# A two-layer decoder trunk on one core: seven products for 12 instead of 8 of the 22 row tiles of the feed-forward down projection

## The chip, the core and the metric

The program runs on one core of a Trainium2 chip. The metric is the device time of one execution in microseconds (us). TensorE (PE in the profile) multiplies matrices, VectorE (DVE) and ScalarE (ACT) work on rows of numbers, GpSimd (POOL) and SyncE (SP) issue transfers (DMAs). Each engine takes the instructions of its own list in the order in which they stand there.

## What is computed

Two layers of a decoder trunk in float32, 512 tokens of 1024 features. Each layer has a feed-forward block, a mixer (a gated recurrence beside attention) and a second feed-forward block. Cut to what matters here:

```python
def swiglu(h, w_gate, w_up, w_down):
    return (jax.nn.silu(h @ w_gate) * (h @ w_up)) @ w_down      # 1024 -> 2816 -> 1024

for l in range(DEPTH):                                            # DEPTH = 2
    h = rms_norm(x, gn[0])
    x = x + 0.5 * rms_norm(swiglu(h, w_ffn1_gate[l], w_ffn1_up[l], w_ffn1_down[l]), gn[1])
    ...                                                           # the mixer
    h = rms_norm(x, gn[4])
    x = x + 0.5 * rms_norm(swiglu(h, w_ffn2_gate[l], w_ffn2_up[l], w_ffn2_down[l]), gn[5])
```

The change is in the last product, `... @ w_down`. It runs four times: two blocks in each of two layers. Its inner dimension, 2816, is 22 tiles of 128 rows.

## The kernel before

**Splitting.** A float32 operand v is held as a pair hi, lo: hi is v rounded to a shorter format (a `copy` on ScalarE, CAST in the profile), lo is the rest v - hi (a subtraction on VectorE). A product takes three matmuls: hi by hi, hi by lo, lo by hi (`mm3`, L381). In another form of the split (`split_dma`, L408) ScalarE writes hi and then -v, and a GpSimd DMA adds v to the latter as it lands; VectorE has no part in it.

**Weights.** `Stream` brings the weights through the core as a list of items. An item is 128 x 1024 numbers: it is loaded by SP into one of W32 = 4 buffers (`w32`), and split into one of WS = 6 pairs `whi`, `wlo`. `ahead` (L342) lets the split run up to `most` items ahead of the one in use; `most` is AHEAD = 3. `quarter` (L255) makes the items of the seven products; the row tiles' second column half lies beside them in tiles of the pool `big` (`b12`, `b22`).

**The down projection.** `down` (L637) multiplies the 22 activation tiles `src` (128 rows x 512 tokens) by `w_down`, into eight accumulators `y[t][h]`: t is a block of 128 tokens, h a half of the 1024 columns. A unit j is two row tiles (2j and 2j+1) of one column half; `both(j, h)` (L672) works it for the four t, 24 matmuls of 512 columns. Eight row tiles by eight accumulators can also be had by seven products of half-sized operands instead of eight (p1 to p7, sums and differences of the quarters of both operands): 8 to 15 are done so, p1 to p7 at four row tiles each.

The order of the matmuls is the program's own order:

1. the lead: units 0 to 3, h = 0, in `down`. While they run, `Late.sums` (L618) forms the activation sums of the seven products, one row pair (8 + i, 12 + i) at a time: `x1` is the split of a quarter, `quarter_sums` (L455) four VectorE instructions that give s and t, of which s is split at once and t later, in `more`. `ready` (L648) splits the row tiles of the units that follow.
2. `quarters` (L772): p1, p6, p2, p7, p5, p4, p3, 24 matmuls each.
3. units 8 to 10, h = 0; then all seven units with h = 1, of which the last four (TAIL) go token block by token block, so that the norm of block t can start while t + 1 is multiplied.
4. while the last block is multiplied, `pre.turn` (L572) transposes the first two normed blocks for the stage that follows.

What sets the order elsewhere: TensorE's list is as written. The other engines' lists are ordered when the program is built, by a scheduler with priorities and a timing model of its own; instructions given to `pin` keep the order in which they are written among each other. Tiles are slots of pools (`big`: 61 slots; accumulators: `acc` 5, `aux` 3), and an instruction that takes a slot waits for the slot's last user.

Of the kernel before, what the change touches and what calls it, by code (L numbers as in the profile page):

```python
# [15 lines left out]
P = 128  # L16
# [22 lines left out]
LEAD = 8  # L39
ORDER = ("p1", "p6", "p2", "p7", "p5", "p4", "p3")  # L40
DMAS = ()
# [4 lines left out]
def trunk(ctx: ExitStack, tc: tile.TileContext, xin, wall, gains, lbT, hgain, sinks, c_dist, c_mask, c_ident, out):  # L46
# [109 lines left out]
    class Stream:  # L156
# [36 lines left out]
        def rows(self, kt, fast):  # L193

            u0 = self.wall

            def pieces(j, h):
                b = [(4 * h + i) * kt + 2 * j for i in range(4)]  # L200
                return [(slice(i * 2 * P, (i + 1) * 2 * P), wall[u0 + n // 8][:, n % 8 * P : (n % 8 + 2) * P]) for i, n in enumerate(b)]

            def unit(j, h):
                c = 2 * j * P
                self.src[self.n] = [(None, wall[u0 + 4 * h : u0 + 4 * h + 4, :, c : c + 2 * P].rearrange("u p c -> p u c"))] if kt == 8 else pieces(j, h)
                self.plain(1)

            j0, later = LEAD // 2 if fast else 0, []
            if fast:
                for j in range(j0):  # L210
                    unit(j, 0)

                u = self.n
                for q in range(2):
                    self.src[u + q] = pieces(j0 + q, 0)
                    self.src[u + 2 + q] = pieces(j0 + 2 + q, 0)
                self.side[u + 1] = [pieces(j0 + q, 1) for q in range(4)]
                for k in ORDER:
                    for q in range(2):
                        it = Item(k, u + q + (2 if k in ("p2", "p4") else 0), 4)  # L220
                        it.base, it.q = u, q
                        self.items.append(it)
                self.t2 = [None, None]
                self.n += 4
                for j in range(j0):
                    later.append(j)
                j0 += 4
            for j in range(j0, kt // 2):
                unit(j, 0)
                later.append(j)  # L230
            for j in later:
                unit(j, 1)
            self.wall = u0 + kt

        def load(self, upto):
            while self.dma < min(upto, self.n):
                w = sb.tile([P, D], F32, tag="w32", name=nm("w32"), bufs=W32)
                u = self.dma
                if isinstance(self.src[u], list):
                    for c, a in self.src[u]:  # L240
                        nc.sync.dma_start(w.rearrange("p (m c) -> p m c", m=4) if c is None else w[:, c], a)  # L241
                else:
                    for c in (slice(0, D // 2), slice(D // 2, D)) if u == 0 else (slice(0, D),):
                        nc.sync.dma_start(w[:, c], wall[self.src[u]][:, c])
                self.raw[u] = w
                self.dma += 1
                if u in self.side:
                    self.b12, self.b22 = [], []
                    for i, ps in enumerate(self.side[u]):
                        v = [big(), big()]  # L250
                        for c, a in ps:
                            nc.sync.dma_start(v[c.start // S][:, c.start % S : c.start % S + 2 * P], a)
                        (self.b22 if i > 1 else self.b12).append(v)

        def quarter(self, it):  # L255

            self.load(it.base + 4)
            q, h = it.q, (slice(0, S), slice(S, D))
            if it.kind in ("p1", "p2", "p5", "p4"):
                w = [self.raw[it.u][:, c] for c in h]  # L260
                if it.kind == "p4":
                    for c in range(2):
                        pin(nc.vector.tensor_tensor(w[c], w[c], self.t2[q][c], op=ALU.add))
            elif it.kind == "p6":

                t = sb.tile([P, D], F32, tag="tt", name=nm("tt"), bufs=2)
                self.t2[q] = w = [t[:, c] for c in h]
                for c in range(2):
                    t1 = self.raw[it.u][:, h[c]]
                    pin(nc.vector.tensor_tensor(t1, t1, self.b12[q][c], op=ALU.subtract))  # L270
                    pin(nc.vector.tensor_tensor(w[c], t1, self.b22[q][c], op=ALU.subtract))
            elif it.kind == "p3":
                w = self.b22[q]
            elif it.kind == "p7":

                w = self.b12[q]
                for c in range(2):
                    pin(nc.vector.tensor_tensor(w[c], w[c], self.b22[q][c], op=ALU.add))
            it.hi = sb.tile([P, D], F32R, tag="whi", name=nm("whi"), bufs=WS)
            it.lo = sb.tile([P, D], F32R, tag="wlo", name=nm("wlo"), bufs=WS)  # L280
            for c in range(2):
                nc.scalar.copy(it.hi[:, h[c]], w[c])  # L282
                if it.kind in DMAS:
                    nc.scalar.mul(it.lo[:, h[c]], w[c], -1.0)
                    nc.gpsimd.dma_start(it.lo[:, h[c]].bitcast(F32), w[c], accum_op=ALU.add)
                else:
                    nc.vector.tensor_tensor(it.lo[:, h[c]], w[c], it.hi[:, h[c]].bitcast(F32), op=ALU.subtract)  # L287
            self.done += 1
            self.flight += 1
            if it.kind in ("p5", "p4"):  # L290
# [106 lines left out]
    def split(src, scale=None, to=None):  # L397

        hi, lo = to or (big(F32R), big(F32R))
        if scale is None:  # L400
            nc.scalar.copy(hi, src)  # L401
# [70 lines left out]
    class Quarters:  # L472
# [4 lines left out]
        def operand(self, n):  # L477
# [4 lines left out]
            return [[v[:, i, :] for v in x[k]] for k in range(4)]  # L482
# [127 lines left out]
    class Late(Quarters):  # L610


        def __init__(self, src, k0):
            self.src, self.k0 = src, k0
            self.x1, self.x56, self.x37, self.t = [], [], [], []
# [12 lines left out]
        def more(self, n):  # L628

            for i in range(len(self.x37), n):  # L630
                self.src[self.k0 + 4 + i] = split(self.src[self.k0 + 4 + i])
                self.x37.append(pair_split(self.t[i], split_dma))

        def raw(self, half, i):
            return [cut(self.src[self.k0 + 4 + k], HALF[half]) for k in range(4)] if i else self.x1

    def down(src, kt, l, n, nxt, fast):  # L637
# [8 lines left out]
        pre = Pre(*nxt) if nxt else None  # L646

        def ready(n):  # L648

            for i in range(min(n, kt)):  # L650
# [6 lines left out]
        def piece(b, t, h, j, i):  # L657
            st = cut(src[2 * j + i], slice(t * P, (t + 1) * P))
            mm3(y[t][h], st, [halves(w, i) for w in b[2:]], 2 * j + i == 0 and not (fast and h and t < 2), 2 * j + i == kt - 1)
# [20 lines left out]
        js = list(range(kt // 2))  # L680
        if fast:
            late = Late(src, LEAD)
            for j in range(LEAD // 2):
                ready(2 * j + EARLY)
                while len(late.x56) < min(4, 8 * (j + 1) / LEAD):
                    late.sums()
                both(j, 0)
            more = quarters(late, y)
            del js[LEAD // 2 : LEAD // 2 + 4]
        for j in js[LEAD // 2 if fast else 0 :]:  # L690
            ready(2 * j + 2 + EARLY)
            both(j, 0)
        if not fast:
            for t in range(TT):
                y[t][1] = aux() if t > 1 else acc()
        fetch()
        last = js[-TAIL:]
        for j in js[:-TAIL]:
            both(j, 1)

        warm = small([P, 1], "warm", 2)
        pin(nc.scalar.activation(out=warm, in_=src[last[0]][0][:, :1].bitcast(F32), func=AF.Sqrt, bias=eps_t, scale=0.0))
# [69 lines left out]
    def quarters(late, y):  # L772
# [3 lines left out]
        def product(n, o, start, stop=True):  # L776
            its = [ws.whole(), ws.whole()]
            for k in range(4):
                for t in range(2):
                    st = cut(late.operand(n)[k], slice(t * P, (t + 1) * P))  # L780
                    it = its[k // 2]
                    mv = [w.rearrange("p (m two c) -> p m two c", two=2, c=P)[:, :, k % 2, :] for w in (it.hi, it.lo)]
                    mm3(o[t], st, mv, start and k == 0, stop and k == 3)
# [12 lines left out]
        late.more(2)  # L796
        p = product(1, two(acc), True)
        p1, u2, u3, c12, c22 = (two(big) for _ in range(5))
        for t in range(2):
            nc.scalar.copy(p1[t], p[t])  # L800
        late.more(4)
# [8 lines left out]
        product(4, [y[t][0] for t in (2, 3)], False, False)  # L810
        for t in range(TT):
            y[t][1] = aux() if t > 1 else acc()
        product(3, [y[t][1] for t in (0, 1)], True, False)
# [72 lines left out]
    def fast(pre, a, start):  # L886
        def early():
            if j == FT - 1:
                for i in range(EARLY):
# [562 lines left out]
```

## Time and profile before

| what | value |
| --- | --- |
| time, median of 3 runs (lowest, highest) | 2100.54 us (2100.14, 2103.34) |
| the profiled execution's own time | 2100.66 us |
| its span, first to last instruction | 2098.9 us |
| PE busy, instructions | 2090.3 us, 13549 |
| DVE busy, instructions | 1550.5 us, 2705 |
| ACT busy, instructions | 1122.4 us, 1899 |
| POOL busy, instructions | 154.2 us, 188 |
| mean granted TensorE clock | 0.999 |

How to read it: a row of the timeline gives start and duration in us, engine, line, operation, what is written and read, the shape, how many were merged, and in brackets the engine's idle time before it and what ended that. A duration is from start to end, and instructions of an engine overlap a little: the distance between two starts is what one costs in a queue. Matmuls overlap most: their ends are modelled, so a busy share near 100% does not mean that every matmul starts as early as it can.

### The profile page before, as it was taken

What the parts mean: (1) busy time and instruction counts of PE and PEld (TensorE: products, weight loads), DVE (VectorE), ACT (ScalarE), POOL (GpSimd) and SP (SyncE); (2) the same over time, 40 slices, a digit from 0 to 9 for tenths busy, and PEclk for the clock granted to TensorE, in tenths of its full rate; (3) what the DMA queues carried; (4) which work ended last, traced back from release to release, by engine and by line L of the source; (5) the groups of instructions that cost most, each with busy time, mean ns of one, the idle gap of its engine ahead of it and who ended that gap; (6) DMA issues with size and microseconds to landing.
All of it is one profiled execution on the core that took longest, in us unless ns stands there. A gap on an engine that the chain in (4) does not pass through costs nothing.

```text
span 2098.9 us, 35207 instructions
## 1 busy us (share of the span) xinstructions
PE 2090.3 (100%) x13549; PEld 1875.3 (89%) x13549; DVE 1550.5 (74%) x2705; ACT 1122.4 (53%) x1899; POOL 154.2 (7%) x188
## 2 busy tenths in 40 slices
PE   9999999999999999999999999999999999999998
PEld 8899988887888999998899998898778989999987
DVE  5877886766776777789587778767687758777884
ACT  6555564456454555556455556554653545555562
POOL 0011000000000011110001110000000000111000
PEclk9999999999999999999999999999999999999999
DMA  8577653312236357774447775632122563677651
GB/s 246 152 181 184 178 157 135 111 61 71 71 101 203 127 122 182 181 198 122 154 114 176 183 181 150 191 120 92 51 81 61 136 193 103 159 182 181 184 160 51
DMA packets 148071, 298.35 MB, mean 142 GB/s; under 512 B 16992, under 2 KB 74816, under 8 KB 147904
## 3 DMA queue, kind: packets, MB, share of 16 engines
q1 hardware_dynamic: 122416, 228.16, 33.2%
q0 software_dynamic: 25344, 67.91, 18.7%
q8 instruction: 106, 1.74, 0.3%
q14 instruction: 61, 0.50, 0.1%
q10 hardware_dynamic: 144, 0.05, 0.0%
HBM read 213.43 MB, written 14.73 MB: 109 GB/s over the span
## 4 chain that ended last, share of the span: by engine, by line
PE 88%; DMA 0%; DVE 0%; ACT 0%; SPq 0%; issue 0%; ACTq 0%
PE acc L115 64%; PE aux L115 22%; PE aux L125 1%; PE acc L125 1%; DMA wlo<-w 0%; DMA w<-wall 0%; SPq L241 0%; DVE s L402 0%; ACT whi L282 0%; DVE s L731 0%; ACT s L600 0%; DVE s L712 0%; DVE s L896 0%; DVE wlo L287 0%; ACT m L895 0%
## 5 line engine op out<-in xcount | busy, mean ns | idle before, releaser
L115 PE MATMUL acc<-s,whi 128*128 128x256 f32 (+1 forms) x4952 | 1059.3, 311 | 0.4 <-ACT whi L325 0.3
L115 PEld LDWEIGHTS acc<-s,whi 128*128 128x128 f32 x4952 | 808.0, 191 | 51.3 <-issue 3.2
L115 PE MATMUL acc<-s,wlo 128*128 128x256 f32 (+1 forms) x2476 | 766.6, 310 | 0.1
L115 PEld LDWEIGHTS acc<-s,wlo 128*128 128x128 f32 x2476 | 472.6, 191 | 25.0 <-DVE wlo L332 0.4
L325 ACT CAST whi<-w 128x1024 fp32r<-128x1024 f32 (+1 forms) x341 | 316.6, 948 | 237.6 <-PE acc L115 95.5
L115 PE MATMUL acc<-whi,s 128*128 128x512 f32 x1264 | 413.6, 393 | 0.1
L325 ACT CAST whi<-tt 128x1024 fp32r<-128x1024 f32 x154 | 161.4, 1048 | 326.5 <-DVE tt L319 184.2
L332 DVE TENSOR_TENSOR wlo<-w,whi 128x1024 fp32r<-128x1024 f32 (+1 forms) x181 | 218.3, 1215 | 151.4 <-ACT whi L325 149.6
L115 PEld LDWEIGHTS acc<-whi,s 128*128 128x128 f32 x1264 | 237.1, 188 | 54.7 <-ACT whi L325 1.6
L332 DVE TENSOR_TENSOR wlo<-tt,whi 128x1024 fp32r<-128x1024 f32 x154 | 188.1, 1221 | 98.8 <-ACT whi L325 98.7
L115 PE MATMUL acc<-wlo,s 128*128 128x512 f32 x632 | 246.4, 390 | 0.0
L115 PE MATMUL aux<-s,whi 128*128 128x256 f32 (+1 forms) x1248 | 230.4, 285 | 0.0
L330 POOL DMA_DIRECT2D wlo<-w x160 | 137.8, 863 | 1258.6 <-ACT wlo L329 704.9
L115 PE MATMUL aux<-whi,s 128*128 128x512 f32 x592 | 196.7, 390 | 0.0
L115 PEld LDWEIGHTS aux<-s,whi 128*128 128x128 f32 x1248 | 195.2, 192 | 1.1 <-issue 0.5
L115 PE MATMUL aux<-s,wlo 128*128 128x256 f32 (+1 forms) x624 | 177.5, 284 | 0.0
L115 PEld LDWEIGHTS acc<-wlo,s 128*128 128x128 f32 x632 | 118.7, 188 | 23.4
L115 PEld LDWEIGHTS aux<-whi,s 128*128 128x128 f32 x592 | 111.1, 188 | 22.8
L329 ACT ACTIVATE wlo<-w 128x1024 fp32r<-128x1024 f32 (+1 forms) x160 | 129.8, 844 | 0.0
L401 ACT CAST s<-s 128x512 fp32r<-128x512 f32 (+1 forms) x164 | 88.4, 580 | 71.5 <-DVE s L460 67.9
L115 PEld LDWEIGHTS aux<-s,wlo 128*128 128x128 f32 x624 | 119.8, 192 | 0.3
L115 PE MATMUL aux<-wlo,s 128*128 128x512 f32 x296 | 115.2, 389 | 0.0
(186 smaller groups left out, 2128.6 us busy)
## 6 DMA issues: line engine op xcount, KB each, us to landing
w<-wall SPq DMA_DIRECT2D x267, 512.0 KB, 3.7
wlo<-w POOLq DMA_DIRECT2D x83, 512.0 KB, 5.5
w<-wall SPq DMA_DIRECT2D x288, 128.0 KB, 3.3
wlo<-w POOLq DMA_DIRECT2D x77, 256.0 KB, 3.3
x_d<-s SPq DMA_DIRECT2D x48, 256.0 KB, 2.1
s<-x_d SPq DMA_DIRECT2D x48, 256.0 KB, 5.5
w<-wall SPq DMA_DIRECT2D x34, 256.0 KB, 3.0
s<-wall SPq DMA_DIRECT2D x64, 128.0 KB, 3.6
```

The source lines that it names most:

```text
L115: nc.tensor.matmul(o, lhsT, rhs, start=start, stop=stop)
L125: nc.tensor.transpose(o, src, ident)
L325: i = nc.scalar.copy(it.hi[:, c], w[:, c])
L329: nc.scalar.mul(it.lo[:, c], w[:, c], -1.0)
L330: nc.gpsimd.dma_start(it.lo[:, c].bitcast(F32), w[:, c], accum_op=ALU.add)
L332: nc.vector.tensor_tensor(it.lo[:, c], w[:, c], it.hi[:, c].bitcast(F32), op=ALU.subtract)
L401: nc.scalar.copy(hi, src)
```

## The change

- The seven products take row tiles 0 to 11 (SEVEN = 12, six row tiles to a product) instead of 8 to 15. The lead is now units 6 to 10 (five, row tiles 12 to 21) with h = 0; no unit with h = 0 comes after the products. With h = 1 the same five units follow, the last four again block by block.
- The products come as p1, p3, p7, p2, p6, p4, p5, with other sums: p1 is added to p6 and p7 at the end, and p3, p2, p4 go straight to accumulators, with three items (36 matmuls) each.
- In the lead `most` is 1 (the item in use and one more), except at its last unit. ScalarE's roundings are pinned there: weights, `x1` and the row tiles of the lead stand on ScalarE in the order in which they are written. The row tiles that the lead splits (`part`) are given up after their unit and split again for h = 1.
- Of the sums, t is split in the lead by `split_dma`; s and the raw row tiles 6 to 11 after p7, also by `split_dma`. Before, s was split in the lead with VectorE.
- y[2][1] and y[3][1] are now `acc`, y[0][1] and y[1][1] `aux`.
- The first four row tiles of the lead are split ahead of it, as before (now tiles 12 to 15).

```diff
-LEAD = 8
-ORDER = ("p1", "p6", "p2", "p7", "p5", "p4", "p3")
+SEVEN = 12
+ORDER = ("p1", "p3", "p7", "p2", "p6", "p4", "p5")
...
         def quarter(self, it):
-            self.load(it.base + 4)
...
+            n, q, h = SEVEN // 4, it.q, (slice(0, S), slice(S, D))
+            self.load(it.base + n if it.kind == "p3" else it.u + 1)
...
             for c in range(2):
-                nc.scalar.copy(it.hi[:, h[c]], w[c])
...
+                i = nc.scalar.copy(it.hi[:, h[c]], w[c])
+                if self.pinned:
+                    pin(i)
+                pin(nc.vector.tensor_tensor(it.lo[:, h[c]], w[c], it.hi[:, h[c]].bitcast(F32), op=ALU.subtract))
...
     class Late(Quarters):
         def sums(self):
-            k = self.k0 + len(self.x56)
-            a = [self.src[i][:, c] for i in (k, k + 4) for c in HALF]
+            k = len(self.x1)
+            a = [self.src[i][:, c] for i in (k, k + self.n) for c in HALF]
             x = big(F32R, [P, 2, S // 2])
-            self.x1.append(split(a[0], to=(x[:, 0, :], x[:, 1, :])))
+            self.x1.append(split(a[0], to=(x[:, 0, :], x[:, 1, :]), hold=pin))
             s, t = quarter_sums(a[0], a[2], a[1], a[3], True)
-            self.x56.append(pair_split(s))
-            self.t.append(t)
+            self.s.append(s)
+            self.x37.append(pair_split(t, split_dma))
             self.src[k] = ()
...
         if fast:
-            late = Late(src, LEAD)
-            for j in range(LEAD // 2):
-                ready(2 * j + EARLY)
-                while len(late.x56) < min(4, 8 * (j + 1) / LEAD):
+            late = Late(src)
+            ws.pinned = True
+            for i, j in enumerate(js):
+                ws.most = 1 if j != js[-1] else AHEAD
+                for k in range(2 * j, min(2 * j + EARLY, kt)):
+                    if k not in part and not isinstance(src[k], tuple):
+                        part[k] = split(src[k], hold=pin)
+                while len(late.x1) < min(late.n, (late.n * (i + 1) + 3) // 4):
                     late.sums()
                 both(j, 0)
-            more = quarters(late, y)
+                for k in (2 * j, 2 * j + 1):
+                    part.pop(k, None)
+            ws.pinned = False
+            more = quarters(late, y, fetch)
...
     def quarters(late, y, fetch):
-        add(u2, product(6, two(aux), True), p1)
-        product(2, [y[t][0] for t in (0, 1)], False, False)
-        add(u3, product(7, two(acc), True), u2)
-        p = product(5, two(aux), True)
-        add(c12, p, u2)
+        product(3, [y[t][1] for t in (0, 1)], True, False)
+        p = product(7, two(acc), True)
+        late.rest()
+        late.more()
+        add(u3, p, p1)
+        product(2, [y[t][0] for t in (0, 1)], False)
+        p = product(6, two(acc), True)
+        add(c12, p, p1)
+        add(u3, p, u3)
+        product(4, [y[t][0] for t in (2, 3)], False)
+        fetch()
+        p = product(5, two(acc), True)
         add(c22, p, u3)
+        add(c12, p, c12)
```

Three places show how the lists move. First ScalarE in the lead, where the weights of a unit are rounded. Before, from the weights of the lead's fourth and last unit (`whi_490`) on; the `L282` rows are the first items of p1, `m_464` is the SiLU of the last gate tile, which ends the stage before, and the rest are activations:

```order
L325 CAST whi_490_2836<-w32_456_2665 128x1024
L401 CAST s_474_2749<-s_108_578 128x512
L282 CAST whi_503_2894<-w32_467_2710 128x512 x2
L282 CAST whi_514_2945<-w32_478_2760 128x512 x2
L895 ACTIVATE m_464_2702<-m_464_2702 128x512
L401 CAST s_498_2875<-s_217_1157 128x256
L401 CAST s_501_2884<-s_499_2878 128x512
L401 CAST s_505_2918<-s_139_711 128x512
L401 CAST s_507_2922<-s_157_804 128x512
```

Now, the same list at the end of the lead's roundings; `whi_535` is the fifth unit's weights, `s_538` and `s_540` its two row tiles (20 and 21), the `L408`/`L409` pairs the split of t (`s_527` and `s_532` for sums 4 and 5 of the six), 256-wide casts the `x1`:

```order
L398 CAST s_521_2985<-s_417_2427 128x512
L398 CAST s_523_2989<-s_437_2560 128x512
L398 CAST s_525_2993<-s_108_578 128x256
L408 CAST s_528_3002<-s_527_2997 128x512
L409 ACTIVATE s_529_3003<-s_527_2997 128x512
L398 CAST s_530_3007<-s_139_711 128x256
L408 CAST s_533_3016<-s_532_3011 128x512
L409 ACTIVATE s_534_3017<-s_532_3011 128x512
L322 CAST whi_535_3027<-w32_467_2710 128x1024
L398 CAST s_538_3054<-s_457_2693 128x512
L398 CAST s_540_3058<-s_497_2880 128x512
```

The weights of the fifth unit stand behind the roundings of five of the six sums; before, the weights of all the lead's units and of p1's two items stood ahead of the sums.

Second, VectorE where the stage before ends (`m_464` again). Before:

```order
L875 TENSOR_TENSOR m_464_2702<-acc_459_2697,s_462_2700 128x2x256
L287 TENSOR_TENSOR wlo_504_2895<-w32_467_2710,whi_503_2894 128x512 x2
L287 TENSOR_TENSOR wlo_515_2946<-w32_478_2760,whi_514_2945 128x512 x2
L877 TENSOR_TENSOR s_463_2701<-acc_460_2698,m_464_2702 128x512
L882 TENSOR_TENSOR m_464_2702<-acc_460_2698,s_463_2701 128x256
L883 TENSOR_TENSOR m_464_2702<-aux_461_2699,s_463_2701 128x512
L896 SCALAR_TENSOR_TENSOR s_493_2868<-m_464_2702 128x512
```

and now:

```order
L891 TENSOR_TENSOR m_464_2702<-acc_459_2697,s_462_2700 128x2x256
L893 TENSOR_TENSOR s_463_2701<-acc_460_2698,m_464_2702 128x512
L898 TENSOR_TENSOR m_464_2702<-acc_460_2698,s_463_2701 128x256
L899 TENSOR_TENSOR m_464_2702<-aux_461_2699,s_463_2701 128x512
L912 SCALAR_TENSOR_TENSOR s_497_2880<-m_464_2702 128x512
L399 TENSOR_TENSOR s_502_2887<-s_80_440,s_502_2887 128x256
L456 TENSOR_TENSOR s_503_2890<-s_177_901,s_80_440 128x256
```

The four subtractions for p1's items have left this place; the sums follow at once.

Third, TensorE where the down projection ends and the next stage starts with four accumulators. Before, from the last matmul of y[3][1] (`aux_603`) on:

```order
L115 MATMUL aux_603_3390<-whi_646_3637,s_621_3454 128x512
L115 MATMUL acc_730_3963<-s_694_3854,whi_666_3691 128x256
L115 MATMUL acc_730_3963<-s_695_3855,whi_666_3691 128x256
L115 MATMUL acc_730_3963<-s_694_3854,wlo_667_3692 128x256
L115 MATMUL acc_731_3964<-s_694_3854,whi_666_3691 128x256
```

and now:

```order
L114 MATMUL acc_662_3695<-whi_667_3710,s_690_3761 128x512
L114 MATMUL acc_759_4052<-s_723_3943,whi_695_3780 128x256
L114 MATMUL acc_759_4052<-s_724_3944,whi_695_3780 128x256
L114 MATMUL acc_759_4052<-s_723_3943,wlo_696_3781 128x256
L114 MATMUL acc_760_4053<-s_723_3943,whi_695_3780 128x256
```

y[3][1] now sits in one of the five `acc`, and the next stage's fourth accumulator, `acc_762`, takes its slot.

More of the change, by code (lines that the diff above doesn't have):

```diff
@@ L276, in quarter @@
                 w = self.b12[q]
-                for c in range(2):
-                    pin(nc.vector.tensor_tensor(w[c], w[c], self.b22[q][c], op=ALU.add))
+                sums(w, w, self.b22[q], ALU.add)
+            elif it.kind == "p6":
+                w = self.t2[q]
+            else:
+                w = raw
+                sums(w, w, self.t2[q], ALU.add)
             it.hi = sb.tile([P, D], F32R, tag="whi", name=nm("whi"), bufs=WS)
@@ L395, in cut, with split @@
         return pair[0][:, c], pair[1][:, c]
-    def split(src, scale=None, to=None):
+    def split(src, scale=None, to=None, hold=lambda i: i):
         hi, lo = to or (big(F32R), big(F32R))
         if scale is None:
-            nc.scalar.copy(hi, src)
+            hold(nc.scalar.copy(hi, src))
             nc.vector.tensor_tensor(lo, src, hi.bitcast(F32), op=ALU.subtract)
@@ L481, in operand @@
             x, i = (self.x56, n - 5) if n in (5, 6) else (self.x37, (n - 3) // 4)
-            return [[v[:, i, :] for v in x[k]] for k in range(4)]
+            return [[v[:, i, :] for v in p] for p in x]
     class First(Quarters):
@@ L646, in down @@
         pre = Pre(*nxt) if nxt else None
+        js = list(range(SEVEN // 2 if fast else 0, kt // 2))
+        part = {}
         def ready(n):
-            for i in range(min(n, kt)):
+            for i in range(2 * js[0], min(n, kt)):
                 if not isinstance(src[i], tuple):
@@ L657, in piece @@
         def piece(b, t, h, j, i):
-            st = cut(src[2 * j + i], slice(t * P, (t + 1) * P))
-            mm3(y[t][h], st, [halves(w, i) for w in b[2:]], 2 * j + i == 0 and not (fast and h and t < 2), 2 * j + i == kt - 1)
+            k = 2 * j + i
+            st = cut(part.get(k) or src[k], slice(t * P, (t + 1) * P))
+            start, stop = k == 2 * js[0], k == kt - 1
+            if fast:
+                start, stop = start and (h == 0 or t > 1), stop and h == 1
+            mm3(y[t][h], st, [halves(w, i) for w in b[2:]], start, stop)
         xt = [[None] * 2 for _ in range(TT)]
@@ L678, in both @@
                 order.poll()
-        js = list(range(kt // 2))
         if fast:
-            late = Late(src, LEAD)
-            for j in range(LEAD // 2):
-                ready(2 * j + EARLY)
-                while len(late.x56) < min(4, 8 * (j + 1) / LEAD):
+            late = Late(src)
[6 more added lines that the diff above has]
+                while len(late.x1) < min(late.n, (late.n * (i + 1) + 3) // 4):
                     late.sums()
                 both(j, 0)
-            more = quarters(late, y)
[L689 to L696, printed above, removed]
+                for k in (2 * j, 2 * j + 1):
+                    part.pop(k, None)
+            ws.pinned = False
+            more = quarters(late, y, fetch)
+        else:
+            for j in js:
+                ready(2 * j + 2 + EARLY)
+                both(j, 0)
+            fetch()
+        for t in range(TT):
+            if not y[t][1]:
+                y[t][1] = (acc if (t > 1) == fast else aux)()
         last = js[-TAIL:]
         for j in js[:-TAIL]:
+            ready(2 * j + 2 + EARLY)
             both(j, 1)
         warm = small([P, 1], "warm", 2)
-        pin(nc.scalar.activation(out=warm, in_=src[last[0]][0][:, :1].bitcast(F32), func=AF.Sqrt, bias=eps_t, scale=0.0))
+        pin(nc.scalar.activation(out=warm, in_=src[2 * last[0]][0][:, :1].bitcast(F32), func=AF.Sqrt, bias=eps_t, scale=0.0))
         left = [TT]
@@ L770, in down, with quarters @@
         return pre
-    def quarters(late, y):
+    def quarters(late, y, fetch):
         def product(n, o, start, stop=True):
-            its = [ws.whole(), ws.whole()]
-            for k in range(4):
+            x = late.operand(n)
+            for k in range(late.n):
+                if k % 2 == 0:
+                    it = ws.whole()
+                mv = [w.rearrange("p (m two c) -> p m two c", two=2, c=P)[:, :, k % 2, :] for w in (it.hi, it.lo)]
                 for t in range(2):
[L780 to L783, printed above, removed]
+                    mm3(o[t], cut(x[k], slice(t * P, (t + 1) * P)), mv, start and k == 0, stop and k == late.n - 1)
                     ws.used((it, 1))
@@ L794, in two @@
             return [f(), f()]
-        late.more(2)
         p = product(1, two(acc), True)
-        p1, u2, u3, c12, c22 = (two(big) for _ in range(5))
+        late.x1 = None
+        p1, u3, c12, c22 = (two(big) for _ in range(4))
         for t in range(2):
             nc.scalar.copy(p1[t], p[t])
-        late.more(4)
-        add(u2, product(6, two(aux), True), p1)
-        product(2, [y[t][0] for t in (0, 1)], False, False)
-        add(u3, product(7, two(acc), True), u2)
-        p = product(5, two(aux), True)
-        add(c12, p, u2)
+        for t in range(2):
+            y[t][1] = aux()
+        product(3, [y[t][1] for t in (0, 1)], True, False)
[8 more added lines that the diff above has]
+        product(4, [y[t][0] for t in (2, 3)], False)
+        fetch()
+        p = product(5, two(acc), True)
         add(c22, p, u3)
[L810 to L813, printed above, removed]
+        add(c12, p, c12)
         return [[(p1, u3)[t // 2][t % 2], (c12, c22)[t // 2][t % 2]] for t in range(TT)]
@@ L888, in early @@
             if j == FT - 1:
-                for i in range(EARLY):
+                for i in range(SEVEN, SEVEN + EARLY):
                     a[i] = split(a[i])
```

96 lines of the change are left out of this document (43 added, 53 removed).

## The prediction

> **What bounds the kernel now.** I read the page first: the share of each engine, then the chain that ended last, then TensorE's waits.
>
> ```profile
> PE 2090.3 (100%) x13549; PEld 1875.3 (89%) x13549; DVE 1550.5 (74%) x2705; ACT 1122.4 (53%) x1899; POOL 154.2 (7%) x188
> PE 88%; DMA 0%; DVE 0%; ACT 0%; SPq 0%; issue 0%; ACTq 0%
> PE acc L125 <- DVE s L731: 2.9, 1, 2.9
> PE aux L115 <- DVE eps_t L138: 1.1, 1, 1.1
> PE acc L115 <- ACT whi L325: 0.3, 1, 0.3
> ```
>
> TensorE is the bound: it waits three times in the whole program, 4.3 us together, at the start and the end. So a matmul taken away is worth its full time, and a wait put anywhere into TensorE's list costs its full length. The question is whether VectorE and ScalarE still deliver in time. That is read in the timeline around one down projection; I use the first, whose lead starts at 240.94. Call that time T.
>
> ```profile
> 240.94 0.40 PE L115 MATMUL acc<-whi,s 128*128 128x512 f32 x1
> 251.85 0.44 PE L115 MATMUL acc<-whi,s 128*128 128x512 f32 x1
> 252.60 0.74 PE L115 MATMUL acc<-whi,s 128*128 128x512 f32 x2
> 263.16 0.39 PE L115 MATMUL acc<-whi,s 128*128 128x512 f32 x1
> 274.04 0.39 PE L115 MATMUL acc<-whi,s 128*128 128x512 f32 x1
> 284.92 0.39 PE L115 MATMUL aux<-whi,s 128*128 128x512 f32 x1
> ```
>
> From 263.16 (start of p1) to 274.04 and 284.92 there are 48 matmuls of 512 columns each: 10.88 us, so **0.2267 us a matmul**. The lead's 96 would end at T + 21.76 = 262.70; p1 starts at 263.16, so the lead loses 0.46 us already, at its third unit (251.85 to 252.60), where the rows' splits are just late. There is no slack in the lead before, and that is where the change adds work.
>
> **What is removed.** A down before has 16 row tiles at 24 matmuls, halves of both columns counted (14 units at 24 = 336), and 7 x 24 = 168 for the products: 504. Now 10 units (240) and 7 x 36 = 252: 492. Twelve fewer in each of four downs, 48 in all: 4 x 12 x 0.2267 = **-10.88 us**. "TensorE: Matmul & The Clock Gate" of the Trainium skill, section "Wait — 56ns, not 53.3ns?", gives 215.7 ns from start to start for 512 columns on a warm array; by it the 48 would be worth 10.35 us, and the rows here are 5% above it.
>
> **The lead, step by step.** Two engines hand the sums back and forth. VectorE, around the end of the stage before and the first sum:
>
> ```profile
> 242.52 0.69 DVE L875 TENSOR_TENSOR m<-acc,s 128x512 f32<-128x512 f32 x1
> 243.12 1.28 DVE L287 TENSOR_TENSOR wlo<-w,whi 128x512 fp32r<-128x512 f32 x2
> 244.67 1.39 DVE L287 TENSOR_TENSOR wlo<-w,whi 128x512 fp32r<-128x512 f32 x2 [0.27 <-ACT whi L282]
> 245.98 0.68 DVE L877 TENSOR_TENSOR s<-acc,m 128x512 f32<-128x512 f32 x1
> 246.70 0.42 DVE L882 TENSOR_TENSOR m<-acc,s 128x256 f32<-128x256 f32 x1
> 247.04 0.68 DVE L883 TENSOR_TENSOR m<-aux,s 128x512 f32<-128x512 f32 x1
> 248.47 0.69 DVE L896 SCALAR_TENSOR_TENSOR s<-m 128x512 f32<-128x512 f32 x1 [0.76 <-ACT m L895]
> 249.08 0.42 DVE L402 TENSOR_TENSOR s<-s,s 128x256 fp32r<-128x256 f32 x1
> 249.42 0.42 DVE L459 TENSOR_TENSOR s<-s,s 128x256 f32<-128x256 f32 x1
> 250.09 0.42 DVE L460 SCALAR_TENSOR_TENSOR s<-s,s 128x256 f32<-128x256 f32 x1
> 250.54 0.42 DVE L462 TENSOR_TENSOR s<-s,s 128x256 f32<-128x256 f32 x1
> 240.78 1.23 DVE L332 TENSOR_TENSOR wlo<-w,whi 128x1024 fp32r<-128x1024 f32 x1 [1.24 <-ACT whi L325]
> 241.92 0.69 DVE L402 TENSOR_TENSOR s<-s,s 128x512 fp32r<-128x512 f32 x1
> ```
>
> By the distances of starts VectorE takes 0.60 for 512 numbers (248.47 to 249.08), 0.34 for 256 (249.08 to 249.42), 0.45 where the next one reads its result (250.09 to 250.54), 0.71 so for 512 (L877 to L882), and 1.14 for 1024. ScalarE:
>
> ```profile
> 239.70 1.05 ACT L325 CAST whi<-w 128x1024 fp32r<-128x1024 f32 x1 [2.19 <-PE aux L115]
> 240.65 0.61 ACT L401 CAST s<-s 128x512 fp32r<-128x512 f32 x1
> 247.81 0.63 ACT L895 ACTIVATE m<-m 128x512 f32<-128x512 f32 x1 [2.47 <-DVE m L883]
> 248.35 0.39 ACT L401 CAST s<-s 128x256 fp32r<-128x256 f32 x1
> 250.60 1.97 ACT L401 CAST s<-s 128x512 fp32r<-128x512 f32 x4 [1.86 <-DVE s L460]
> 258.45 0.93 ACT L401 CAST s<-s 128x512 fp32r<-128x512 f32 x2 [1.96 <-DVE s L460]
> 264.89 0.62 ACT L411 CAST s<-s 128x512 fp32r<-128x512 f32 x1
> 265.41 0.63 ACT L412 ACTIVATE s<-s 128x512 fp32r<-128x512 f32 x1
> ```
>
> ScalarE takes 0.95 for 1024, 0.52 for 512, 0.31 for 256 (0.93 for one of each, the last at its full 0.39). It starts 0.09 after VectorE's result (250.09 + 0.42 to 250.60), VectorE 0.03 after ScalarE's (247.81 + 0.63 to 248.47).
>
> With these I play the new lists through:
>
> 1. The four L287 are gone from VectorE's place between L875 and L877. L877 can start 0.71 after L875, at 243.23 instead of 245.98: **2.75 us earlier**. L883 ends at 244.97, the SiLU runs from 245.06, and sum 0 is done at 248.21 (249.08 to 250.96 takes 1.88, from 246.33).
> 2. Then each sum is a loop: t's two roundings on ScalarE (0.09 + 0.52 + 0.52), x1 of the next sum, which stands behind them (0.39 + 0.03), and on VectorE x1's rest, L457 and L459 (0.34 + 0.45 + 0.42). 2.76 us. Sum 1 is done at 250.97.
> 3. Row tiles 16 and 17 stand between t and the next x1: two roundings more (1.04) and two subtractions. ScalarE rounds t from 251.06, the tiles at 252.10 and 252.62, and VectorE subtracts until 253.44 and 254.04. TensorE wants them for its third unit at T + 10.88 = 251.82. Its first matmul needs the rounding that ends at 252.72, the third the first rest, and this unit starts **1.23 late**.
> 4. Sum 2 is done at 255.85 (4.88 with two tiles between). Tiles 18 and 19 follow, rounded by 258.1; the fourth unit starts at 251.82 + 1.23 + 5.44 = 258.49, with its first tile rounded at 257.6: in time, by some 0.6 with the rests.
> 5. Sum 3 is done at 260.71, sum 4 at 263.47. Only then come t's two roundings, and behind them the **weights of the fifth unit**, pinned there because `most` is 1: 264.60 to 265.65. Tile 20 is rounded by 266.17; VectorE's rest of the weights ends at 266.92, those of tiles 20 and 21 at 267.52 and 268.12.
> 6. TensorE wants the fifth unit at 262.70 + 1.23 = 263.93. The six matmuls of its first token block follow these results one by one, the last after 268.12, so the block ends at 268.49; without any wait in the lead it would end at 262.70 + 6 x 0.2267 = 264.07. **The lead loses 4.42 us** and had lost 0.46: +3.96 a down. The bounds: if sums 2 to 4 each ran 0.3 shorter, 3.5; each 0.3 longer, 5.3.
> 7. The sixth sum (VectorE done 269.9) and t's roundings stand ahead of p1's weights. ScalarE rounds them from 271.02, VectorE's second half of the rest ends at 272.97, and TensorE asks for it at 268.49 + 18 x 0.2267 + 0.23 = 272.80: **+0.27** with the 0.09 for the handover. Bounds 0 and 0.6, since a few tenths of lateness in 6 shift the asking too.
>
> After p1 each product has 36 x 0.2267 = 8.16 us of TensorE's time for three items (6 casts, 3.1 us, and 6 to 18 subtractions, 3.6 to 10.8 us), and the heavier ones, p7 and p6, are followed by p2 and p5 or p4, that need less. Played through, operands of p3 to p5 stand ready 3 us and more ahead, so I cost the products' additions, the six raw tiles and six s by GpSimd (12 transfers off VectorE's list) and the loads on SP at nothing. If that cover were gone by 1 us in one product it would cost 4 us in all. The row tiles that are split twice (six, 6 x 0.60 on VectorE) fall between h = 1 units of 5.44 us: nothing, too.
>
> **The turn.** Three downs are followed by a stage with four `acc` at once.
>
> ```profile
> 357.42 0.40 PE L115 MATMUL acc<-s,whi 128*128 128x256 f32 x2
> 357.77 0.40 PE L115 MATMUL acc<-s,whi 128*128 128x256 f32 x2
> 358.23 0.68 DVE L712 TENSOR_TENSOR s<-aux,s 128x512 f32<-128x512 f32 x1
> ```
>
> Before, y[3][1] is in `aux`, and VectorE's read of it, ending at 358.91, holds nobody up. Now it is in `acc`, and the next stage's fourth accumulator takes its slot. TensorE asks after nine matmuls, at 357.42 + 9 x 0.12 = 358.50 (three take 0.35). The read ends 0.41 after that at the least, and 1.4 after if VectorE, with the re-splits in its tail, is 1 us later. I take **+0.65**, nearer the first, since the old row is the only one shown; three times, +1.95. After the last down no stage follows.
>
> **The sum.** Per down -2.72 + 3.96 + 0.27 = +1.51, four times +6.04; the turn +1.95; together +8.0. The profiled execution took 2100.66, 0.12 from the median of 2100.54, so 2108.7 by the one and 2108.5 by the other: **2108.6 us**.
>
> **Rivals.**
>
> *Faster: the lead keeps up.* The removed 10.88 and the old loss of 4 x 0.46 = 1.84 come back, and p1 is on time: about 2088. For it speaks that VectorE starts the sums 2.75 us earlier. It decides at the fifth unit's weights: they would have to be rounded some 3 us earlier, before sum 3's roundings. The list has them behind sum 4's, and 2.76 a sum follows from rows alone. Chance 0.08.
>
> *No change.* If half of the lead's wait is hidden (x1 and t taking less of the loop than the rows say) and the turn costs 0.4: 4 x (-2.72 + 1.98 + 0.1) + 1.2 = -1.4, so 2099; up to 2104 with the turn at its upper end. Chance 0.12.
>
> *Slower still: the clock.* TensorE waits over 2 us before the fifth unit and has only six matmuls in the next 2 us. The end of the program shows what a pause does:
>
> ```profile
> 2093.23 1.63 PE L125 MATMUL acc<-ident,s 128*128 128x128 f32 x8 [2.85 <-DVE s L731]
> 2094.00:2095.00 1.00, 0.86 (x4) 0.45 (x4) 0.62 (x1) 0.10 (x1) 0.00 (x0) 0.61 0.00 0
> 2095.00:2096.00 1.00, 0.00 (x0) 0.00 (x0) 0.00 (x0) 0.48 (x1) 0.00 (x0) 0.50 0.38 121
> ```
>
> After a wait of 2.85 us the granted clock falls to 0.61 and 0.50, some 3.8 us after the last dense matmul. If it did so in the lead and stayed at half for as long, 1.9 us of work would be lost each time: four times 7.6, about 2116. Against it: the pause is shorter, and the old profile has no other such slice. Chance 0.12. "TensorE: Matmul & The Clock Gate" of the Trainium skill, section "What's actually happening", says that the clock drops to half after an idle window of about 3.4 us and comes back after a busy one as long; by that rule the drop needs a longer pause than the one I work out, and one trip would cost about 1.7 us. The trace's end agrees with the drop to half.
>
> That the change does not do what it says can be left out: twelve matmuls a down are gone from TensorE's list.
>
> **Chances and range.** The main case has 0.68, its own range 2105 to 2113 from the bounds of 6, 7 and the turn. The range 2101 to 2116 adds the upper half of "no change" and the clock; outside lie the faster rival and the tails. No change means within 0.2%, 4.2 us, about what a measurement of this kernel tells apart: 0.12. Faster 0.08, slower 0.80.
>
> **What would show it.** In the new profile, TensorE's waits should name row splits (ACT L398, DVE L399) and the fifth unit's weights (DVE L329) in four places, 4 us and more together at each; the weights' cast L322 should start some 23.7 us after the lead's start; p1 should start near T + 31.6, where five units without a loss (120 matmuls) would make T + 27.2; a small wait on DVE L725 should stand at the next stage's start, three times; matmuls should number 13501. The prediction is wrong if p1 starts before T + 29, or if waits show in the products, or if slices of the granted clock go below 9.

## The result, and the profile after

| | before | after |
| --- | --- | --- |
| time, median | 2100.91 us (4 runs, 2100.14 to 2103.34) | 2125.53 us (4 runs, 2124.27 to 2127.51) |
| ratio, 95% interval | | 1.0116, 1.0099 to 1.0134 |
| profiled execution: span | 2098.9 us | 2123.5 us |
| matmuls | 13549 | 13501 |

The change makes the kernel 24.6 us slower; 8.0 were forecast. The page of the changed kernel, with the chain, and its TensorE waits (line: us in total, times, longest):

```profile
PE 2095.3 (99%) x13501; PEld 1869.7 (88%) x13501; DVE 1589.3 (75%) x2801; ACT 1181.4 (56%) x2035; POOL 202.6 (10%) x244
PE 68%; DVE 7%; ACT 5%; DMA 3%; issue 2%; SPq 1%; ACTq 0%; DVEq 0%; POOL 0%; POOLq 0%
PE acc L114 <- ACT s L398: 12.9, 8, 2.7
PE aux L114 <- DVE s L399: 4.1, 7, 0.8
PE acc L114 <- DVE s L588: 1.1, 3, 0.4
PE acc L114 <- DVE wlo L329: 0.9, 4, 0.2
```

PE's busy time rises by 5.0 us with 48 matmuls fewer: the busy share does not show the slow clock (6.3 us, below), nor all of a stop, since a matmul alone counts as 0.39 us and one in a dense row costs 0.2267. The chain leaves TensorE for VectorE, ScalarE and loads, which it hardly did before.

**The lead** (first down, T = 241.16; PE, then ScalarE around the fifth unit):

```profile
253.11 0.50 PE L114 MATMUL acc<-whi,s 128*128 128x512 f32 x1 [0.88 <-ACT s L398]
266.83 0.51 PE L114 MATMUL acc<-whi,s 128*128 128x512 f32 x1 [2.23 <-ACT s L398]
267.57 0.50 PE L114 MATMUL acc<-wlo,s 128*128 128x512 f32 x1 [0.23 <-DVE wlo L329]
264.18 0.62 ACT L408 CAST s<-s 128x512 fp32r<-128x512 f32 x1 [1.59 <-DVE s L459]
265.23 1.03 ACT L322 CAST whi<-w 128x1024 fp32r<-128x1024 f32 x1
266.17 1.44 ACT L398 CAST s<-s 128x512 fp32r<-128x512 f32 x3
```

The third unit waits for row splits, the fifth for its weights and rows, which ScalarE rounds at T + 24.07 and T + 25.01, behind t of the fifth sum. This is the forecast place (T + 23.7 for the weights).

**The clock.** One-microsecond windows of the second down, busy us (count) of PE, PEld, DVE, ACT, POOL, then the granted clock:

```profile
968.00:969.00 1.00, 0.41 (x1) 0.19 (x1) 0.95 (x1) 1.00 (x4) 0.24 (x1) 1.00 0.24 43
969.00:970.00 1.00, 0.76 (x3) 0.25 (x2) 1.00 (x3) 0.37 (x2) 0.00 (x0) 0.79 1.08 186
970.00:971.00 1.00, 1.00 (x3) 0.81 (x4) 1.00 (x3) 0.00 (x0) 0.00 (x0) 0.50 0.68 170
972.00:973.00 1.00, 1.00 (x4) 0.80 (x3) 0.28 (x1) 0.64 (x2) 0.00 (x0) 0.50 0.59 166
973.00:974.00 1.00, 1.00 (x6) 0.77 (x5) 0.00 (x0) 1.00 (x3) 0.20 (x1) 1.00 0.00 0
```

After the fifth unit's wait the clock is at half from 969.58 (0.79 is 0.42 us at half) to 973.0, although TensorE works again: these windows touch three or four matmuls each, 973:974 at full clock six.

**The units with h = 1** (first down; PE, then ScalarE; last the fourth down's ScalarE):

```profile
342.46 0.73 PE L114 MATMUL aux<-whi,s 128*128 128x512 f32 x2 [0.78 <-DVE s L399]
344.20 0.73 PE L114 MATMUL aux<-whi,s 128*128 128x512 f32 x2 [0.78 <-DVE s L399]
331.70 1.05 ACT L322 CAST whi<-w 128x1024 fp32r<-128x1024 f32 x1 [5.12 <-DMA w<-wall]
335.98 1.05 ACT L322 CAST whi<-w 128x1024 fp32r<-128x1024 f32 x1 [1.62 <-DMA w<-wall]
336.94 2.18 ACT L398 CAST s<-s 128x512 fp32r<-128x512 f32 x4
339.02 1.04 ACT L322 CAST whi<-w 128x1024 fp32r<-128x1024 f32 x1
339.96 1.13 ACT L398 CAST s<-s 128x512 fp32r<-128x512 f32 x2
2086.76 3.21 ACT L398 CAST s<-s 128x512 fp32r<-128x512 f32 x6
```

The six row tiles that are split a second time are rounded from 336.94 on, behind weights whose loads are late. TensorE goes block by block there and asks for all six within one block of 5.4 us, from 336.2. In the fourth down they are rounded in one go, and nothing waits.

**The turn:**

```profile
366.17 0.47 PE L114 MATMUL acc<-s,whi 128*128 128x256 f32 x2 [0.35 <-DVE s L588]
366.67 0.50 PE L114 MATMUL acc<-s,whi 128*128 128x256 f32 x2
365.94 0.68 DVE L725 TENSOR_TENSOR s<-acc,s 128x512 f32<-128x512 f32 x1
```

The next stage starts at 364.95 with three matmuls to an accumulator. The third accumulator (366.17) waits for L588, which writes the rest half of a normed block from an accumulator. The fourth starts at 366.67, as soon as L725 has read its slot (365.94 + 0.68 = 366.62). That is 0.64 after 364.95 + 9 x 0.12, and 0.66 in the other two turns. The list of waits names L588 alone, because before the fourth accumulator hardly any idle time is left; but L725 comes last, and by itself it would hold TensorE to the same point.

**Where 24.6 us come from.** I list each matmul's start against the one before, less 0.2267 us (0.12 for 256 columns), and add what is over 0.1:

| down | lead | slow clock | h = 1 | turn | down, start to end, after less before |
| --- | --- | --- | --- | --- | --- |
| 1 | 4.8 | 1.55 | 3.5 | 0.6 | 123.79 - 116.48 = +7.3 |
| 2 | 4.2 | 1.54 | 1.9 | 0.6 | 121.47 - 116.06 = +5.4 |
| 3 | 4.7 | 1.59 | 1.05 | 0.6 | 121.09 - 116.16 = +4.9 |
| 4 | 5.7 | 1.59 | 0 | none | +4.7 |
| sum | 19.4 | 6.3 | 6.4 | 1.8 | 22.3 |

19.4 + 6.3 + 6.4 less the 10.9 of the removed matmuls and 0.5 that the old leads lost is 20.7 of the 22.3; most of the rest is slips under 0.1 us. With the turns' 1.8 it is 24.1 of 24.6.

### The profile page after: what moved, and what is told of

Its sections match the earlier page's. It is cut to its first block, busy times and chain, and to the rows that moved or that the text cites. A ratio compares the mean times of both kernels' runs of the same rounds, so it can differ in the third digit from the quotient of the medians.

```text
span 2123.5 us, 35581 instructions
## 1 busy us (share of the span) xinstructions
PE 2095.3 (99%) x13501; PEld 1869.7 (88%) x13501; DVE 1589.3 (75%) x2801; ACT 1181.4 (56%) x2035; POOL 202.6 (10%) x244
## 4 chain that ended last, share of the span: by engine, by line
PE 68%; DVE 7%; ACT 5%; DMA 3%; issue 2%; SPq 1%; ACTq 0%; DVEq 0%; POOL 0%; POOLq 0%
PE acc L114 52%; PE aux L114 14%; DMA w<-wall 3%; DVE wlo L329 1%; PE aux L124 1%; DVE wlo L277 1%; ACT whi L322 1%; ACT s L409 1%; ACT s L408 1%; DVE s L399 1%; ACT whi L274 1%; SPq L233 1%; DMA s<-s 1%; DVE s L255 0%; PE acc L124 0%
## 5 line engine op out<-in xcount | busy, mean ns | idle before, releaser
L114 PE MATMUL acc<-whi,s 128*128 128x512 f32 x1344 | 443.1, 397 | 13.2 <-ACT s L398 12.9
L322 ACT CAST whi<-w 128x512 fp32r<-128x512 f32 (+1 forms) x325 | 299.6, 942 | 175.5 <-PE acc L114 107.9
L114 PEld LDWEIGHTS acc<-whi,s 128*128 128x128 f32 x1344 | 253.9, 189 | 76.7 <-ACT s L398 16.3
L329 DVE TENSOR_TENSOR wlo<-w,whi 128x1024 fp32r<-128x1024 f32 (+1 forms) x165 | 199.0, 1214 | 103.0 <-ACT whi L322 102.2
L114 PE MATMUL acc<-wlo,s 128*128 128x512 f32 x672 | 264.3, 393 | 0.9 <-DVE wlo L329 0.9
L114 PE MATMUL aux<-whi,s 128*128 128x512 f32 x480 | 161.6, 395 | 4.1 <-DVE s L399 4.1
L114 PEld LDWEIGHTS acc<-wlo,s 128*128 128x128 f32 x672 | 127.3, 189 | 27.7 <-DVE wlo L329 2.2
L114 PEld LDWEIGHTS aux<-whi,s 128*128 128x128 f32 x480 | 90.1, 189 | 26.4 <-DVE s L399 7.8
L399 DVE TENSOR_TENSOR s<-s,s 128x512 fp32r<-128x512 f32 (+1 forms) x148 | 86.8, 620 | 27.2 <-ACT s L398 27.1
L912 DVE SCALAR_TENSOR_TENSOR s<-m 128x512 f32<-128x512 f32 x69 | 47.8, 692 | 76.1 <-ACT m L911 75.7
```

What stands on the lines that cost most here:

```text
L114: nc.tensor.matmul(o, lhsT, rhs, start=start, stop=stop)
L322: i = nc.scalar.copy(it.hi[:, c], w[:, c])
L329: nc.vector.tensor_tensor(it.lo[:, c], w[:, c], it.hi[:, c].bitcast(F32), op=ALU.subtract)
L399: nc.vector.tensor_tensor(lo, src, hi.bitcast(F32), op=ALU.subtract)
L912: nc.vector.scalar_tensor_tensor(z, m[:, 0:2, :], -1.0, m[:, 2:4, :], op0=ALU.mult, op1=ALU.mult)
```

## Experiments

Theory 2 is the prediction's: the sums fill ScalarE and VectorE, and what stands behind five of them is late. Theory 1 blames only the weights' place. The re-splits and the clock are asked after separately.

**Weights three items ahead**

```diff
-                ws.most = 1 if j != js[-1] else AHEAD
+                ws.most = AHEAD
```

> The changed kernel, with the weights of the lead rounded three items ahead instead of one (`most` = AHEAD in the whole lead); the sums stay where they are. Theory 1 (the fifth unit waits because its weights stand behind five sums): its weights come early, the wait of 3.3 us there and the drop of the clock behind it go, four downs gain 4 x (3 to 5), about 2107. Theory 2 (it waits because the sums, 2.76 us each and 4.9 with two row tiles, fill ScalarE and VectorE; whatever stands behind five of them is late, and row tiles 20 and 21 stand there too): the weights' roundings go in ahead of the early sums and push everything behind them, so the third unit loses some 2.5 instead of 1.3, the fifth still 3.3; 2125 to 2132.

Measured 2127.52 us (2 runs), as theory 2 has it. From start to start the four leads lose 24.5 us instead of 19.4. TensorE's wait for row splits grows, and ScalarE in the first lead shows why:

```profile
PE acc L114 <- ACT s L398: 16.2, 8, 2.7
251.56 1.03 ACT L322 CAST whi<-w 128x1024 fp32r<-128x1024 f32 x1
252.50 1.44 ACT L398 CAST s<-s 128x512 fp32r<-128x512 f32 x3
```

The fifth unit's weights are in time at 251.56, but go ahead of the third unit's rows, and the fifth unit still waits for its own. The weights' place by itself is not the cause; theory 1 falls.

**Sums late**

```diff
-                ws.most = 1 if j != js[-1] else AHEAD
+                ws.most = AHEAD
...
-                while len(late.x1) < min(late.n, (late.n * (i + 1) + 3) // 4):
+                while len(late.x1) < (1, 1, 2, 4, 6)[i]:
```

> The changed kernel with `most` = AHEAD and the six sums put off: 1, 1, 2, 4, 6 of them formed by the lead's units 1 to 5 instead of 2, 3, 5, 6, 6. Theory 2 (too many sums ahead of the fifth unit's operands): no wait in the lead, so the drop of the clock behind it does not come either; each down gains 4.0 to 4.5 and 1.6: 2101 to 2104, with the waits for the split-again row tiles at h = 1 still there. Theory 3 (the lead's roundings are late because ScalarE's fixed order waits for something else, a load or the accumulator): the waits stay, within 3 us of the changed kernel's 2125.5.

Measured 2109.95 us (4 runs; ratio to before 1.0043, 1.0026 to 1.0059), 15.6 less than the changed kernel, but 6 us above the 2101 to 2104 expected. The wait for row splits in the lead is gone from the list; what stands there:

```profile
PE aux L114 <- DVE s L399: 5.6, 10, 0.8
PE acc L114 <- DVE wlo L277: 1.8, 6, 0.3
```

The four leads lose 0.7 us together, and the granted clock drops once, after the h = 1 waits of the third down, instead of four times. But of 24.1 us (lead 19.4, three slow clocks 4.7) 8.5 are given back. TensorE comes some 5 us earlier now; from start to start it loses 9.5 instead of 6.4 us at h = 1 and, new, 4.8 in the products. (The rows above, 5.6 and 1.8, count only what shows as idle.) With the 0.7 left in the leads that is about the 8.5. Since the weights' place alone gained nothing, what the leads gain comes from the sums' place.

**Row tiles split again before p5**

```diff
-            more = quarters(late, y, fetch)
+            more = quarters(late, y, lambda: (ready(kt), fetch()))
```

> The changed kernel with the six row tiles split again before p5, ahead of the loads that the down's end asks for, instead of between the units with h = 1. If their late splitting makes the waits at h = 1 (3.4, 1.9 and 1.1 us in the first three downs, none in the fourth) and the slow clock after the first: 6.4 to 8 us less, about 2118. If the weights' late loads make them: no more than 2 us less.

Measured 2114.17 us (2 runs), 11.4 less; 6.4 to 8 were expected. All waits at h = 1 are gone, and L588 no longer stands in the list. The last two lines are windows with the granted clock at half, in the first and the third lead:

```profile
PE acc L114 <- ACT s L398: 12.6, 8, 3.3
PE acc L114 <- DVE wlo L329: 0.5, 2, 0.2
266.00:269.00 3.00, 2.94 (x7) 1.87 (x7) 2.97 (x8) 0.46 (x2) 0.00 (x0) 0.50 0.83 191
1311.00:1317.00 6.00, 6.00 (x14) 4.23 (x14) 4.20 (x10) 3.01 (x7) 0.86 (x1) 0.50 0.57 126
```

So the waits at h = 1, worth 6.4, came from the second splits' place on ScalarE. The slow clock is not saved with them: the clock is at half for as long as before, 4 x 3.41 us, now once in the first lead, twice as long in the third, once in the fourth and not in the second. The profiled execution is 10.6 us shorter. Beside the 6.4 the leads' waits are worth 1.4, the turns 0.9 (the fourth accumulator is still 0.36 late, after L725), the clock 0.4, and 0.7 lies ahead of the first down, which the edit does not touch; the last 0.8 are slips and what I can't assign.

**Both**

> Both edits: sums late with weights three ahead, and the row tiles split again before p5. If lead, clock and h = 1 are the whole loss, what is left is 48 matmuls less (-10.9), the lead's old loss (-0.5) and about 2 us at the turns: 2090 to 2094, faster than both kernels.

Measured 2103.42 us (10 runs; 1.0013, 1.0004 to 1.0023): not faster than before. TensorE's waits, ScalarE at p2's third item, and SP's waits from 280 to 300:

```profile
PE acc L114 <- DVE s L725: 3.6, 4, 1.0
PE acc L114 <- DVE wlo L277: 2.3, 8, 0.3
294.86 0.62 ACT L274 CAST whi<-w 128x512 fp32r<-128x512 f32 x1 [2.73 <-DMA w<-wall]
296.87 0.62 ACT L274 CAST whi<-w 128x512 fp32r<-128x512 f32 x1 [1.39 <-DMA w<-wall]
SPq L233 <- DVE t L255: 24.1, 3, 20.4
```

Without the lead's loss the products come due earlier, and a chain shows that it had covered: VectorE's sums of p7 (L255) give up the weight buffers, SP loads p2's items into them, ScalarE stands at the third of these, and the splits of s and p6's items queue behind. VectorE ends late, and its reads of the accumulators (L725) too.

**Both, and a fifth weight buffer**

```diff
-W32, WS, AHEAD, TAIL, PLAIN, FIRST, EARLY, LATE = 4, 6, 3, 4, 4, 7, 4, 8
+W32, WS, AHEAD, TAIL, PLAIN, FIRST, EARLY, LATE = 5, 6, 3, 4, 4, 7, 4, 8
...
-SLOTS = 61
+SLOTS = 59
```

> Both edits of before (sums late with weights three ahead; row tiles split again before p5), and a fifth buffer for loaded weights (W32 = 5; `big` gives up two of its 61 slots). In the run without it TensorE lost some 2 us a down in the products: ScalarE stood at p2's third item, whose load waits for a buffer that VectorE's sums of p7 give up, and p6's items queued behind it. If that chain is the rest, the waits on p2, p6 and p4 shrink and the time comes to 2096 to 2099, faster than both kernels. If VectorE's own load in the products is the rest, no change from 2103.4 within 2.

Measured **2094.54 us** (6 runs; 0.9968, 0.9956 to 0.9980): faster than both kernels, 1.5 us below the expected range. In the four downs TensorE waits no more than the first two lines; the third is ScalarE at p2's items:

```profile
PE acc L114 <- DVE wlo L277: 1.2, 4, 0.3
PE acc L114 <- ACT whi L322: 0.5, 1, 0.5
289.41 3.22 ACT L274 CAST whi<-w 128x512 fp32r<-128x512 f32 x6
```

p2's six roundings run in one go, where ScalarE stood twice for a load without the buffer. SP itself waits as long as before (24.5 us from 280 to 300), but the loads are there when ScalarE asks.

The first down takes 114.39 us from the lead's start to the next stage (116.48 before). The chain over the buffers was the rest, but for 2.6 us that p7 still loses from start to start in the four downs.

**The kernel before with the fifth buffer**

> The kernel before with the same fifth buffer and 59 slots, as the control: it has no wait for loads in its downs, so no gain, within 2 us of 2100.6; if the fifth buffer by itself were worth more, it would show here.

Measured 2117.76 us (4 runs; 1.0079, 1.0065 to 1.0093), 16 us slower than the kernel before beside it (2101.57), where I had expected nothing.

```profile
PE acc L115 <- ACT s L401: 8.9, 4, 3.0
243.47 0.79 PE L115 MATMUL acc<-whi,s 128*128 128x512 f32 x1 [2.95 <-ACT s L401]
239.04 1.14 ACT L282 CAST whi<-w 128x512 fp32r<-128x512 f32 x2 [1.83 <-PE aux L115]
242.80 2.18 ACT L401 CAST s<-s 128x512 fp32r<-128x512 f32 x4
```

p1's weights have a buffer earlier and are rounded (L282, 239.04 on) ahead of the rows of the lead's first unit (L401, 242.80), for which TensorE waits; the slow clock follows in all four downs. The changed kernel with the buffer alone was not run. Here the buffer costs time, so it is not a gain in every kernel: what a buffer is worth depends on what it lets go ahead on ScalarE.

**x tiles fetched after the products**

```diff
-        fetch()
         p = product(5, two(acc), True)
...
             more = quarters(late, y, fetch)
+            fetch()
```

> The changed kernel with `fetch` (the norm's row and the eight x tiles, nine transfers on SP) issued after the products, not before p5. If these transfers, which stand on SP's list ahead of the last units' weights and wait 17.6 us for a buffer, make the weights late and so the row tiles behind them, the waits at h = 1 (6.4 us) shrink: about 2119. If the order on ScalarE alone sets them (row tiles behind weights that come late for want of a buffer), no more than 2 us either way.

Measured 2123.44 us (2 runs, 2121.63 and 2125.25); the changed kernel's four lie between 2124.27 and 2127.51, so no difference is shown. TensorE's waits:

```profile
PE acc L114 <- ACT s L398: 14.8, 8, 3.2
PE aux L114 <- DVE s L399: 1.8, 3, 0.6
PE aux L114 <- ACT s L398: 0.9, 3, 0.3
```

At h = 1 2.7 us are waited for instead of 4.1. The edit also moved the second splits on ScalarE (all six behind the fourth weights), so it doesn't separate transfers from order: inconclusive on what part the transfers have. That the waits at h = 1 go when the splits stand earlier was shown above.

## Why the prediction was wrong

The direction held, the size did not: +24.6 against +8.0, outside the range. Of the 16.6 us between them the second splits are 6.4, the clock 6.3, the new leads 1.7 and the old leads 1.3; the rest are small terms. By its steps:

- **48 matmuls less, -10.88:** right; 13501 are left, at 0.2267 us.
- **The lead, steps 1 to 6, 4.42 a down:** right in place and cause, and near in size. Measured 4.8, 4.2, 4.7 and 5.7, at the third unit and the fifth as played through; the fourth lies above my bound of 5.3, and together they are 1.7 us over. The late sums took it away. What it was set against was wrong: I gave all four old leads the first one's 0.46, and together they lost about 0.5. That is 1.3 us of the miss.
- **p1's start, +0.27 a down:** 0.2 in the first, none that can be told in the others. Small either way.
- **The turn, 3 x 0.65:** right, in size and cause. The fourth accumulator starts 0.64, 0.66 and 0.66 late, just after L725. What I did not foresee is that the third waits for L588 inside that time; VectorE works through these instructions one after the other.
- **"The row tiles that are split twice ... fall between h = 1 units of 5.44 us: nothing":** wrong, and the step that failed worst. It measured 6.4 us, and the early second splits removed it. I priced their VectorE time and spread it over units; but the last four units go block by block, so all six are due within one block, and they stood on ScalarE behind weights that waited 5.1 and 1.6 us for loads.
- **The clock:** I named the mechanism, priced it at 1.9 a time and 7.6 in all, and gave it 0.12 as a rival to the main case. It came once in each down, 1.54 to 1.59 each, 6.3 in all: in three downs behind the lead's wait, which I forecast myself, and in the first behind the waits at h = 1, which I did not. My argument against it, that the pause is shorter than the one at the program's end, did not hold: 2.6 us were enough in the second down, while 2.4 were not in the first. A part of it should have stood inside the sum. The sign that I named, a slice of the granted clock below 9, could not show it: a slice is 53 us long, and 3.4 us at half leave it at 0.97.
- **Products at nothing:** right for the changed kernel only because TensorE came late. With the lead mended the chain over the weight buffers cost some 2 us a down.

## What to carry to other kernels

When a step is priced at nothing, look at when its results are *due*, not at how much room the engine has on average: work that is done twice must be ready for the moment at which the consumer walks over all of it at once, and its place behind a load on an in-order engine counts more than its duration. A forecast wait of TensorE of 2 us or more can bring a slow clock, as it did in three of the four leads here (1.5 to 1.6 us each); put its price into the sum, with the chance that it comes. After each mended wait expect the next: here lead, second splits and buffers had to be mended together before the 48 matmuls could be seen.

## What the hardware showed that I had not expected

The slow clock keeps a grid. Its starts in the changed kernel, from the shares of these windows (start = end of the window, less twice what is missing to 1):

```profile
344.00:345.00 1.00, 0.80 (x3) 0.67 (x4) 1.00 (x3) 0.00 (x0) 0.00 (x0) 0.97 0.82 279
1321.00:1322.00 1.00, 1.00 (x4) 0.82 (x3) 1.00 (x4) 0.00 (x0) 0.00 (x0) 0.58 0.79 231
2020.00:2021.00 1.00, 0.77 (x2) 0.19 (x1) 1.00 (x3) 0.56 (x2) 0.00 (x0) 0.94 1.10 193
```

The starts are 344.94, 1321.16 and 2020.88, with 969.58 from above. The distances, 624.64, 351.58 and 699.72, are 183, 103 and 205 times 3.4133 us, to within 0.01 us. Each lasts one such step. I cut five traces (the changed kernel and four of the experiments, both ways of the lead's wait among them) into these steps and added up the matmuls' time in each: every step filled to 0.38 or less at full clock was followed by half clock, none that was filled to 0.42 or more, and between 0.39 and 0.40 both occurred. In the first down the lead's wait of 2.4 us (2.9 with the stops behind it) fell across two steps, of which the first was filled to 0.42, and the clock held; in the second one of 2.6 fell into one step, filled to 0.13, and it dropped. So it depends on where a wait falls in the step, and the step does not start with the program: counted from the first instruction, the grid lies at 0.19 us here, and at 3.02 in the run with the row tiles split again early (its first drop is at 265.84). The Trainium skill, "TensorE: Matmul & The Clock Gate", section "What's actually happening", gives a free-running window of 3413 ns; the trace agrees to the digit. Where the section speaks of an idle window, a window filled to 0.38 was idle enough here.
